# Sample attention of a hybrid layer: keys transposed in 32x32 blocks on VectorE, scores by sixteen 32x32 TensorE tiles

## The chip, the cores and the metric

The kernel runs on one core of a Trainium2 chip. The metric is the time of one launch in microseconds on the device. The engines are named as in the profile: PE is TensorE, PEld its weight loads, DVE is VectorE, ACT is ScalarE, POOL is GpSimd, SP is SyncE.

## What is computed

One layer of a hybrid decoder: 1024 prompt tokens and 8 sample sequences of 8 new tokens each. Half of the mixing width is gated linear attention (GLA), half is multi-head latent attention (MLA) with 4 heads, 256 latent channels and 64 rotary ones; then an output projection and a gated convolutional FFN. The change lies in one part, the attention of the sample tokens over a paged cache of 8192 rows per sequence:

```python
s = einsum('bthl,bsl->bhts', ql, kv) + einsum('bthr,bsr->bhts', qr, kr)
p = softmax(s * scale)
o_lat = einsum('bhts,bsl->bthl', p, kv)
# b 8 sequences, t 8 tokens, h 4 heads, s 8192 keys, l 256, r 64, all float32
```

## The kernel before

The program has four stretches: norms and input projection (to about 318 us of the trace), a mixed stretch, then output projection and FFN (from about 966 us). In the mixed stretch two generators are run side by side: `mla_sample` (lines 1143 to 1235) and `main`, which does the prompt's queries, then GLA, then the prompt's attention. Each yields a number that stands for its share of the work, and whoever is behind goes next. A scheduler of the framework then fixes the order of the instructions of every engine when the program is built; each engine runs its own queue in that order and waits on semaphores.

`mla_sample` runs over 8 sequences and 4 steps each, 32 steps in all, of 2048 keys in two halves. Per half, POOL issues two gathers: L, 128 partitions by 8 keys by 256 latent channels (line 1166, five buffers), and R, the 64 rotary channels of the same keys (line 1167, three buffers). PE transposes L and R in 20 blocks of 128x128 (line 1176) into the PSUM tile kps (two buffers), four blocks to a bank, and ACT copies each bank to KT or KR (line 1178). The scores S fill one bank: the 32 queries (4 heads by 8 tokens) times 512 keys for each quarter of the keys' partitions, four quarters on the 128 partitions, by four column tiles of 128x32 (lines 1186 and 1188). DVE takes the maximum of each partition (rm, line 1191), brings the four quarters together (mg, lines 1194 and 1198) and writes one negated maximum per query back to all quarters (nm, line 1201). ACT takes the exponential p (line 1204) and the factor al for the old sums (line 1207). DVE transposes p in 32x32 blocks (pt, line 1215), PE multiplies by L in 16 products of 128x32 (O, line 1220), and DVE adds to the running sum (on, lines 1223 and 1225). A sequence ends with two small products that add the quarters (fps and lps). float32 products of TensorE appear in the trace as two records each, transposes as one.

KT, KR and S have one buffer each, but O has a bank of its own, so the keys of a step are transposed while the step before still is at its exponentials and O.

Of the kernel before, what the change touches and what calls it, by code (L numbers as in the profile page):

```python
# [10 lines left out]
F32 = mybir.dt.float32  # L11
# [3 lines left out]
AF = mybir.ActivationFunctionType  # L15
# [24 lines left out]
def _consts():  # L40
# [24 lines left out]
    # the rows of a modulation: four parts of nine in steps of 32, then the bias  # L65
# [28 lines left out]
class Rows:  # L94
    """the transposes of all tokens' rows, in two parts each, by groups of tokens"""
# [10 lines left out]
class Kernel:  # L106
# [128 lines left out]
    def ada_section(self, sec, wp, pp, bufs, evac, rp=None):  # L235
# [9 lines left out]
                # four products side by side  # L245
# [60 lines left out]
    def gate(self, k, gvec, gp, name, gb):  # L306
        """gate rows times the norm's gain, for prompt and sample tokens: [128, 2, 1024]"""
# [18 lines left out]
    def to_T(self, xp, pp, xn, h, i, slot, nraw=3, eng=None, both=None):  # L326
        """xn: the normalized rows of tile i; their transposes, modulated, into h"""
# [24 lines left out]
    def phase1(self):  # L352
# [3 lines left out]
        with ExitStack() as es:  # L356
# [37 lines left out]
            # the sample tokens' two parts side by side  # L394
# [22 lines left out]
            def gates():  # L417
                """the forget gates"""
# [18 lines left out]
            def ada():  # L437
                """the other parts of the modulation, a little after each of the products"""
# [19 lines left out]
            # low-rank gate input and query latent  # L458
# [20 lines left out]
            # latents and rotary keys  # L479
# [24 lines left out]
            # GLA queries and keys, transposed  # L504
# [19 lines left out]
            # indices of the sixteenths of pages, by partition  # L524
# [8 lines left out]
            # values and output gates  # L533
# [18 lines left out]
    def rope(self, xp, out, x, tab, h):  # L552
        """out, x: [n, h, 64]; tab [n, 2, 64]"""
# [42 lines left out]
    def gla_group(self, G, cp, bp, pm, g):  # L596
# [16 lines left out]
        # the forget gates' running sums within blocks  # L613
# [11 lines left out]
        # intra-block scores, by levels  # L625
        # odd blocks of 64 on the upper partitions, where their values are
# [54 lines left out]
        # decayed queries and keys  # L681
# [60 lines left out]
        # output norm and gate  # L742
# [7 lines left out]
    def head_norm(self, bp, o, m, nh, gg=None):  # L750
        """o [m, x, y] in place: rows of 128 normalized, times gg [128, 128] if given"""
# [11 lines left out]
    def gla_sample(self, cp, pm, qe, ke, dec, v, at2, o_sb):  # L763
# [9 lines left out]
        # the sums of even and odd sequences side by side  # L773
# [29 lines left out]
    def outer(self, out, k, v):  # L803
        """the heads' sums of keys times values, two heads side by side"""
# [15 lines left out]
    def mla_weights(self, mp, pp):  # L820
# [5 lines left out]
        # the first head's first  # L826
# [77 lines left out]
    def sample_queries(self, zs, xs, ds, es2):  # L904
        """the sample tokens' queries, and the prompt's last ones"""
# [819 lines left out]
```

## Time and profile before

| what | value |
|---|---|
| median of 3 runs | 1889.26 us (1887.93 to 1892.58) |
| the profiled execution, its own time as the trace gives it, first to last instruction (span) | 1894.2 us |
| PE busy | 1815.7 us, 96% |
| DVE, ACT, POOL busy | 939.5, 709.2, 527.4 us |
| mean granted clock of TensorE | 0.984 |

The time of an engine is the sum of what it was busy with, not of what it held up; the views by window, by line and by time tell these apart. PE rows and PEld rows overlap. PE's busy time counts a matmul from its start to its end, and pipelined matmuls overlap, so the time that a group of products takes is best read from the timeline, where a run of them stands as one row.

### The profile page before, as it was taken

Reading aid. Unit: us, or ns where it says so; the run is one execution under the profiler, and the core shown is the slowest. Engines: PE = TensorE matmul, PEld = TensorE weight load, DVE = VectorE, ACT = ScalarE, POOL = GpSimd, SP = SyncE. Lnnn points to the kernel's source line nnn. Section 1 sums busy time; section 2 is a strip of 40 time slices with the busy share of each in tenths; the row PEclk is TensorE's granted clock in tenths of the full one; section 3 lists DMA queues with packets and bytes.
Section 4 is the critical chain, followed back from the end, with each engine's and each line's share of the span. In section 5 each row is a group of like instructions: output and inputs, shape, how many; then the busy total and the mean of one; then the engine's idle time right before and its main releaser. Section 6 shows DMA issues by size and latency. Waiting matters only on the chain.

```text
span 1894.2 us, 30775 instructions
## 1 busy us (share of the span) xinstructions
PE 1815.7 (96%) x12403; PEld 1502.5 (79%) x12403; DVE 939.5 (50%) x1680; ACT 709.2 (37%) x1398; POOL 527.4 (28%) x567
## 2 busy tenths in 40 slices
PE   6999999998998899999999999999999999999998
PEld 3888767764555567776679999999999999888787
DVE  4740334355676445554557755555555554623433
ACT  3451112464456556756633422222222222323322
POOL 2640101243334323232102123333333332202221
PEclk8999999999989999999999999999999999999999
DMA  8155553565454744545445331111121212744563
GB/s 312 68 171 180 187 160 111 192 206 180 169 183 159 250 160 150 188 138 180 159 145 176 101 98 68 61 64 63 68 70 69 70 62 70 246 115 114 155 188 94
DMA packets 170617, 265.26 MB, mean 140 GB/s; under 512 B 18277, under 2 KB 118693, under 8 KB 162282
## 3 DMA queue, kind: packets, MB, share of 16 engines
q1 hardware_dynamic: 156138, 179.39, 29.6%
q0 software_dynamic: 14336, 83.89, 12.7%
q8 instruction: 98, 1.61, 0.3%
q14 instruction: 45, 0.37, 0.1%
HBM read 221.49 MB, written 41.75 MB: 139 GB/s over the span
## 4 chain that ended last, share of the span: by engine, by line
PE 83%; DVE 6%; DMA 5%; ACT 3%; issue 2%; POOL 1%; SPq 1%; DVEq 0%; POOLq 0%; ACTq 0%
PE ups L140 9%; PE ups L142 9%; PE ups L141 9%; PE kps L1176 6%; PE yps L142 4%; PE yps L140 4%; PE yps L141 4%; PE zps L140 3%; PE O L1220 3%; PE zps L142 3%; PE zps L141 3%; PE S L1186 3%; PE y L142 2%; PE y L140 2%; PE y L141 2%
## 5 line engine op out<-in xcount | busy, mean ns | idle before, releaser
L140 PE MATMUL ups<-gh,uhi 128*128 128x384 f32 (+1 forms) x1056 | 347.2, 329 | 0.3 <-DVE hraw L343 0.3
L141 PE MATMUL ups<-gl,uhi 128*128 128x384 f32 (+1 forms) x1056 | 346.7, 328 | 0.0
L142 PE MATMUL ups<-gh,ulo 128*128 128x384 f32 (+1 forms) x1056 | 346.5, 328 | 0.0
L1514 DVE TENSOR_SCALAR cv<-u,vt 128x1024 f32<-128x1024 f32 (+1 forms) x88 | 133.2, 1534 | 216.3 <-ACT u L1504 179.4
L140 PEld LDWEIGHTS ups<-gh,uhi 128*128 128x128 f32 x1056 | 198.3, 188 | 0.7 <-DVE hraw L343 0.6
L142 PEld LDWEIGHTS ups<-gh,ulo 128*128 128x128 f32 x1056 | 198.3, 188 | 0.1
L141 PEld LDWEIGHTS ups<-gl,uhi 128*128 128x128 f32 x1056 | 198.3, 188 | 0.0
L1176 PE MATMUL kps<-ident,L 128*128 128x128 f32 x1024 | 159.9, 286 | 22.4 <-ACT KT L1178 16.2
L1178 ACT COPY KT<-kps 128x512 f32<-128x512 f32 x256 | 145.8, 590 | 82.8 <-PE kps L1176 77.5
L1176 PEld LDWEIGHTS kps<-ident,L 128*128 128x128 f32 x1024 | 113.8, 143 | 78.8 <-issue 42.5
L121 POOL TENSOR_TENSOR ulo<-uraw,uhi 128x2048 fp32r<-128x2048 f32 x24 | 111.4, 4642 | 207.5 <-ACT uhi L1342 204.6
L1504 ACT COPY u<-ups 128x384 f32<-128x384 f32 (+1 forms) x130 | 57.6, 444 | 279.2 <-PE ups L142 279.2
L142 PE MATMUL yps<-uhi,gl 128*128 128x512 f32 x341 | 133.3, 392 | 5.0 <-DVE gl L121 5.0
L140 PE MATMUL yps<-uhi,gh 128*128 128x512 f32 x341 | 133.1, 391 | 0.0
L141 PE MATMUL yps<-ulo,gh 128*128 128x512 f32 x341 | 133.0, 390 | 0.0
L121 DVE TENSOR_TENSOR gl<-graw,gh 128x1408 fp32r<-128x1408 f32 x31 | 59.1, 1908 | 129.3 <-ACT gh L1561 129.3
L1167 POOL DMA_INDIRECT R<-cache_krope,idx x64 | 66.1, 1033 | 181.6 <-PE kps L1176 148.5
L1342 ACT CAST uhi<-uraw 128x2048 fp32r<-128x2048 f32 (+1 forms) x38 | 70.8, 1865 | 94.4 <-PE ups L141 66.9
L1561 ACT CAST gh<-graw 128x1408 fp32r<-128x1408 f32 (+1 forms) x35 | 45.8, 1310 | 158.1 <-PE yps L141 128.6
L1166 POOL DMA_INDIRECT L<-cache_latent,idx x64 | 61.5, 961 | 138.9 <-PE O L1220 68.4
L140 PE MATMUL zps<-whi,hh 128*128 128x512 f32 (+2 forms) x256 | 96.1, 375 | 0.0
L142 PE MATMUL zps<-whi,hl 128*128 128x512 f32 (+2 forms) x256 | 94.2, 368 | 0.8 <-DVE hl L121 0.8
(443 smaller groups left out, 3799.1 us busy)
## 6 DMA issues: line engine op xcount, KB each, us to landing
wraw<-w_ada SPq DMA_DIRECT2D x48, 512.0 KB
uraw<-w_ffn_up SPq DMA_DIRECT2D x22, 1024.0 KB
graw<-s_g SPq DMA_DIRECT2D x32, 704.0 KB
s_g<-gl SPq DMA_DIRECT2D x22, 544.0 KB
uraw<-w_ffn_down SPq DMA_DIRECT2D x10, 1024.0 KB
xt<-x_prompt SPq DMA_DIRECT2D x16, 512.0 KB
wraw<-w_in SPq DMA_DIRECT2D x12, 512.0 KB
uraw<-w_o SPq DMA_DIRECT2D x4, 1024.0 KB
```

Source lines behind the costliest of these rows:

```text
L121: eng.tensor_tensor(out, x, hi.bitcast(F32), ALU.subtract)
L140: mm(out, wh, xh, start=start, stop=False)
L141: mm(out, wh, xl, start=False, stop=False)
L142: mm(out, wl, xh, start=False, stop=stop)
L1166: nc.gpsimd.indirect_dma_start(L.rearrange("p j l -> p (j l)"), None, cl, io)
L1167: nc.gpsimd.indirect_dma_start(R.rearrange("p j l -> p (j l)"), None, ck, io)
L1176: nc.tensor.transpose(ps[:, k], x, self.ident)
L1178: nc.scalar.copy(KT[:, q // 2, j0:j0 + 4] if q < 4 else KR[:, 4 * half:4 * half + 4], ps)
L1186: nc.tensor.matmul(S[r], Q[:, c], KT[:, c, :, r], start=(c == 0), stop=False)
L1342: self.nc.scalar.copy(hi, raw)
L1504: copy(u[:, 2 + c0:2 + c0 + m], ps[:, 0:m])
L1514: nc.vector.tensor_scalar(yv[z], sh(2)[z], self.cw2[:, ch:ch + 1], self.cb[:, ch:ch + 1], ALU.mult, ALU.add)
```

## The change

The keys are no longer transposed on PE. DVE transposes L and R where they lie, in blocks of 32x32, by three instructions per half (lines 1177 and 1179 of the changed file): 128x1024 elements twice, 128x512 once. After this, partition 32x+i holds channel 32c+i of the keys that lay on partitions 32x to 32x+31, for ten chunks c of 32 channels. The queries are laid out to match: Qd holds, for each of the ten chunks, the same 32 rows on all four partition groups; it is made once, by twelve products with a replicating matrix `rep` and twelve copies. The scores are then sixteen tiles of 32x32 for each chunk (x the row group and the PSUM bank, g the column group), 160 products of 128 columns per step, into four banks.

The maximum is kept for each of the 128 partitions by itself: a reduction with negation (line 1192) and, from a sequence's second step, a minimum with the old one (line 1194); mg and its copies leave the step. p is transposed on PE by four 128x128 transposes (line 1210) with one ACT copy (line 1212). O is as before, with another order of the products. At the end of each sequence the four quarters' maxima are brought together, and their factor f scales the selecting matrix (lines 1228 to 1246).

The pools: S now is a tile of four banks with one buffer, and the transposed p, O and the end of the sequence are tiles of the same tag, so they use the same four banks one after the other. kps and its two banks are gone. L has six buffers instead of five, R two instead of three, and KT three (of a half each) instead of one.

```diff
+            rep = dq.tile([P, 4, 4, 32], F32, name="rep")
+            nc.vector.tensor_copy(rep, self.ident.rearrange("p (x o a) -> p x o a", x=4, o=1).broadcast_to([P, 4, 4, 32]))
...
+            for c in range(8):
+                ps = pq.tile([P, 4, 8, 8], F32, name="qps", tag="Q")
+                nc.tensor.matmul(ps.rearrange("p h b t -> p (h b t)"), rep[:, c % 4], qs[:, c // 4].rearrange("p h n -> p (h n)"), start=True, stop=True)
+                (nc.vector.tensor_copy if c % 2 else nc.scalar.copy)(Qd[:, c].rearrange("p b h t -> p h b t"), ps)
...
-                    for q in range(5):
-                        ps = psK.tile([P, 4, P], F32, name="kps", tag="K")
-                        for k in range(4):
-                            x = L[:, 4 * (q % 2) + k, q // 2 * P:q // 2 * P + P] if q < 4 else R[:, 2 * k:2 * k + 2].rearrange("p j r -> p (j r)")
-                            nc.tensor.transpose(ps[:, k], x, self.ident)
-                        j0 = 8 * half + q % 2 * 4
-                        nc.scalar.copy(KT[:, q // 2, j0:j0 + 4] if q < 4 else KR[:, 4 * half:4 * half + 4], ps)
-                        yield 0.5
+                    K = bp.tile([P, 10, 8, 32], F32, name="KT", tag="KT", bufs=3)
+                    for h in range(2):
+                        j = slice(4 * h, 4 * h + 4)
+                        nc.vector.transpose(K[:, 0:8, j].rearrange("p c j k -> p j c k"), L[:, j].rearrange("p j (c k) -> p j c k", k=32))
+                        yield 1.0
+                    nc.vector.transpose(K[:, 8:10].rearrange("p c j k -> p j c k"), R.rearrange("p j (c k) -> p j c k", k=32))
+                    yield 0.5
...
+                S = psS.tile([P, 4, 512], F32, name="S", tag="S")[:, :, 0:P]
+                for c in range(10):
                     for g in range(4):
-                        r = slice(32 * g, 32 * g + 32)
-                        if c < 2:
-                            nc.tensor.matmul(S[r], Q[:, c], KT[:, c, :, r], start=(c == 0), stop=False)
-                        else:
-                            nc.tensor.matmul(S2[r, c - 2], Q[:, c], KR[:, :, r], start=False, stop=(c == 3))
+                        for x in range(4):
+                            r = slice(32 * x, 32 * x + 32)
+                            nc.tensor.matmul(S[32 * g:32 * g + 32, x], Q[r, c], Ks[g // 2][r, c, 4 * (g % 2):4 * (g % 2) + 4].rearrange("p j k -> p (j k)"),
+                                             start=(c == 0), stop=(c == 9))
...
+                nc.vector.tensor_reduce(nm, S, AX.XY, ALU.max, negate=True)
+                if nmo is not None:
+                    nc.vector.tensor_tensor(nm, nm, nmo, ALU.min)
...
-                nc.vector.transpose(pt, p)
+                SO = psS.tile([P, 4, 512], F32, name="S", tag="S")
+                pps = SO[:, 0].rearrange("p (j q) -> p j q", j=4)
+                for j in range(4):
+                    nc.tensor.transpose(pps[:, j], p[:, j], self.ident)
+                nc.scalar.copy(pt, pps)
+                O = SO[:, 1, 0:LAT]
```

How the queues stand, in the stretch beside the prompt's attention. PE's queue of the kernel before, around the scores of one step (kps, S and O belong to the sample attention; sps, pt and olps are the prompt's scores, its transposed weights and its products with the latents):

```order
L1176 MATMUL kps<-ident,R 128x128 x4
L1186 MATMUL S<-KT,Qd 32x512 x4
L1176 MATMUL kps<-ident,L 128x128 x4
L1122 MATMUL pt<-ident,ol 128x128 x2
L1188 MATMUL S<-KR,Qd 32x8x32 x8
L1176 MATMUL kps<-ident,L 128x128 x8
L1107 MATMUL pt<-ident,p 128x128 x3
L1176 MATMUL kps<-ident,L 128x128 x4
L1176 MATMUL kps<-ident,R 128x128 x4
```

The scores of a step stand there in pieces, with transposes of the next keys and work of the prompt between them. PE's queue of the changed kernel at such a place, with all 160 products of a step in a row:

```order
L1086 MATMUL sps<-causal,identr 128x128
L140 MATMUL olps<-pth,vh 128x256
L1187 MATMUL S<-KT,Qd 32x128 x160
L141 MATMUL olps<-ptl,vh 128x256
L142 MATMUL olps<-pth,vl 128x256
L140 MATMUL olps<-pth,vh 128x256
L141 MATMUL olps<-ptl,vh 128x256
L142 MATMUL olps<-pth,vl 128x256
L1114 MATMUL pt<-ident,p 128x128 x3
```

Further on in the same step come the four transposes of p and then O, with the prompt's products between them:

```order
L140 MATMUL olps<-pth,vh 128x256
L1210 MATMUL S<-ident,p 128x128 x4
L141 MATMUL olps<-ptl,vh 128x256
L142 MATMUL olps<-pth,vl 128x256
L140 MATMUL olps<-pth,vh 128x128
L141 MATMUL olps<-ptl,vh 128x128
L142 MATMUL olps<-pth,vl 128x128
L1218 MATMUL S<-L,pt 32x256 x16
```

What moved: the keys' transposes are gone from between the prompt's products, the scores stand in one block, and the prompt's products that follow a block wait behind it. The number of products in a row differs from step to step; in the steps beside GLA the block is also cut in places. GLA's last work stands in the twelfth step of the changed order, and the last two steps have next to no work of `main` beside them.

DVE's queue of the kernel before, over one step:

```order
L1191 TENSOR_REDUCE rm<-S 128x1
L1194 COPY mg<-rm 32x1 x4
L1198 TENSOR_REDUCE mg<-mg 32x1
L1201 TENSOR_SCALAR nm<-mg 32x1 x4
L1091 SCALAR_TENSOR_TENSOR ls<-ls,al,l_8149 128x1
L121 TENSOR_TENSOR ptl<-pt,pth 128x384
L1081 TENSOR_REDUCE nm<-sps 128x1
L1215 STREAM_TRANSPOSE pt<-p 128x512
L1081 TENSOR_REDUCE nm<-sps 128x1
L1209 SCALAR_TENSOR_TENSOR ln<-ln,al,rs 128x1
```

DVE's queue of the changed kernel from the first half's transposes of a step to the sum ln:

```order
L1177 STREAM_TRANSPOSE KT<-L 128x4x8x32 x2
L1179 STREAM_TRANSPOSE KT<-R 128x8x2x32
L1192 TENSOR_REDUCE nm<-S 128x1
L1177 STREAM_TRANSPOSE KT<-L 128x4x8x32 x2
L1179 STREAM_TRANSPOSE KT<-R 128x8x2x32
L1132 TENSOR_TENSOR ob<-pt,ri 128x256
L1194 TENSOR_TENSOR nm<-nm 128x1
L121 TENSOR_TENSOR Kl<-sps,Kh 128x512 x2
L757 TENSOR_REDUCE hms<-hsq 128x2
L1202 SCALAR_TENSOR_TENSOR ln<-ln,al,rs 128x1
```

What moved: the six transposes of the keys stand three before the reduction over S and three behind it, ahead of the minimum that ACT's exponential waits for; the copies of the maxima and the transpose of p are gone.

## Rows read from the trace of the kernel before

**Rows 1.** The page: engines' busy time over the span; then the view of cores.

```profile
PE 1815.7 (96%) x12403; PEld 1502.5 (79%) x12403; DVE 939.5 (50%) x1680; ACT 709.2 (37%) x1398; POOL 527.4 (28%) x567
...
core 0: 1894.2 us, clock 0.984
```

**Rows 2.** Windows: start:end, length, busy us (instructions) of each engine, clock, DMA share, GB/s.

```profile
318.00:405.00 87.00, 81.05 (x681) 62.91 (x679) 35.26 (x111) 41.72 (x92) 28.94 (x28) 0.98 0.59 199
405.00:630.00 225.00, 201.15 (x2085) 125.98 (x2088) 142.03 (x361) 127.22 (x274) 87.60 (x97) 0.95 0.53 179
630.00:966.00 336.00, 320.30 (x2756) 223.26 (x2744) 172.10 (x492) 201.08 (x484) 86.81 (x112) 0.99 0.51 173
```

**Rows 3.** Lines, 318 to 966 us, old transposes, their copies, scores: count, busy us, mean ns, idle.

```profile
L1176 PE MATMUL kps<-ident,L 128*128 128x128 f32 x1024 | 159.9, 286 | 22.4 <-ACT KT L1178 16.2 <-ACT KR L1178 2.6 <-issue 1.7
L1176 PE MATMUL kps<-ident,R 128*128 128x128 f32 x256 | 42.2, 289 | 1.1 <-ACT KT L1178 0.9
L1178 ACT COPY KT<-kps 128x512 f32<-128x512 f32 x256 | 145.8, 590 | 82.8 <-PE kps L1176 77.5 <-PE O L1220 2.0 <-issue 0.9
L1178 ACT COPY KR<-kps 128x512 f32<-128x512 f32 x64 | 37.7, 588 | 26.3 <-PE kps L1176 26.2
L1186 PE MATMUL S<-KT,Qd 128*32 128x512 f32 x512 | 75.4, 611 | 0.6 <-ACT p L1204 0.6
L1188 PE MATMUL S<-KR,Qd 128*32 128x256 f32 x512 | 40.9, 385 | 0.0
```

**Rows 4.** Lines, same stretch: the maximum, the transposed weights, and O's matmuls and loads.

```profile
L1191 DVE TENSOR_REDUCE rm<-S 128x1 f32<-128x512 f32 x32 | 22.0, 686 | 22.2 <-PE S L1188 18.4 <-PE kps L1176 3.7
L1194 DVE COPY mg<-rm 32x1 f32<-32x1 f32 x128 | 18.1, 142 | 2.0
L1198 DVE TENSOR_REDUCE mg<-mg 32x1 f32<-32x5 f32 (+1 forms) x32 | 4.6, 144 | 0.9
L1201 DVE TENSOR_SCALAR nm<-mg 32x1 f32<-32x1 f32 x128 | 18.4, 144 | 2.2
L1215 DVE STREAM_TRANSPOSE pt<-p 128x512 f32<-128x512 f32 x32 | 22.7, 710 | 14.1 <-ACT p L1204 12.9 <-ACT KT L1178 0.8
L1220 PE MATMUL O<-L,pt 128*32 128x256 f32 x1024 | 68.8, 387 | 2.6 <-DVE pt L1215 1.6 <-issue 0.8
L1220 PEld LDWEIGHTS O<-L,pt 128*32 128x32 f32 x1024 | 31.3, 110 | 27.5 <-issue 5.9 <-DVE pt L1215 3.2 <-ACT KT L1178 0.4
```

**Rows 5.** Timeline, 784 to 798 us: start, duration, engine, operation [idle before].

```profile
784.64 0.71 ACT L1204 ACTIVATE p<-S,nm 128x512 f32<-128x512 f32 x1
785.47 0.71 DVE L1215 STREAM_TRANSPOSE pt<-p 128x512 f32<-128x512 f32 x1
787.10 1.93 PE L1220 MATMUL O<-L,pt 128*32 128x256 f32 x32
788.97 1.09 PE L1176 MATMUL kps<-ident,L 128*128 128x128 f32 x8
789.16 0.48 DVE L1225 SCALAR_TENSOR_TENSOR on<-on,al,O 128x256 f32<-128x256 f32 x1 [1.29 <-PE O L1220]
790.73 0.66 PE L1176 MATMUL kps<-ident,L 128*128 128x128 f32 x4 [0.45 <-issue]
793.04 1.07 PE L1186 MATMUL S<-KT,Qd 128*32 128x512 f32 x8
797.35 1.07 PE L1188 MATMUL S<-KR,Qd 128*32 128x256 f32 x16
```

**Rows 6.** Timeline of PE at 477 us: 64x64 tiles on two row groups and two column groups.

```profile
477.01 1.09 PE L716 MATMUL ops<-v,att 64*64 64x128 f32 x16
```

**Rows 7.** The instructions of two lines on DVE that take 1024 columns: min/median/max ns.

```profile
L323 DVE TENSOR_SCALAR rt<-xt,rstd x9: 739/747/754, 997.0 to 1094.7; 128x1024 f32<-128x1024 f32 x8, 64x1024 f32<-64x1024 f32 x1
...
L1428 DVE TENSOR_TENSOR xt<-rt,xt x9: 1208/1218/1226, 993.3 to 1089.3; 128x1024 f32<-128x1024 f32 x8, 64x1024 f32<-64x1024 f32 x1
```

**Rows 8.** Windows: the stretch with the lowest clock among these stages.

```profile
440.00:560.00 120.00, 104.10 (x1118) 67.31 (x1114) 81.81 (x195) 60.77 (x126) 43.79 (x47) 0.90 0.50 173
```

More of the change, by code (lines that the diff above doesn't have):

```diff
@@ L1181, in mla_sample @@
-                S2 = S.rearrange("p (j two k) -> p two j k", two=2, k=32)
-                for c in range(4):
-                    for g in range(4):
-                        r = slice(32 * g, 32 * g + 32)
-                        if c < 2:
-                            nc.tensor.matmul(S[r], Q[:, c], KT[:, c, :, r], start=(c == 0), stop=False)
-                        else:
-                            nc.tensor.matmul(S2[r, c - 2], Q[:, c], KR[:, :, r], start=False, stop=(c == 3))
-                yield 4.4
@@ L1190, in mla_sample @@
-                rm = bp.tile([P, 1], F32, name="rm", tag="rm")
-                nc.vector.tensor_reduce(rm, S, AX.X, ALU.max)
-                mg = mnext or bp.tile([32, 5], F32, name="mg", tag="mg", bufs=3)
-                for g in range(4):
-                    nc.vector.tensor_copy(mg[:, g:g + 1], rm[32 * g:32 * g + 32])
-                first = pc == 0
-                mnext = bp.tile([32, 5], F32, name="mg", tag="mg", bufs=3)
-                mnew = mnext[:, 4:5]
-                nc.vector.tensor_reduce(mnew, mg[:, 0:4 if first else 5], AX.X, ALU.max)
+                    K = bp.tile([P, 10, 8, 32], F32, name="KT", tag="KT", bufs=3)
@@ L1206, in mla_sample @@
+                if nmo is not None:
                     al = bp.tile([P, 1], F32, name="al", tag="al")
@@ L1212, in mla_sample @@
                     lrun = rs
[L1213 to L1220 removed]
+                nmo = nm
+                SO = psS.tile([P, 4, 512], F32, name="S", tag="S")
+                pps = SO[:, 0].rearrange("p (j q) -> p j q", j=4)
+                for j in range(4):
+                    nc.tensor.transpose(pps[:, j], p[:, j], self.ident)
+                pt = bp.tile([P, 4, P], F32, name="pt", tag="pt")
+                nc.scalar.copy(pt, pps)
+                O = SO[:, 1, 0:LAT]
+                for j in range(4):
+                    for g in range(4):
+                        r = slice(32 * g, 32 * g + 32)
+                        nc.tensor.matmul(O[r], pt[:, j, r], Ls[g // 2][:, 4 * (g % 2) + j], start=(j == 0), stop=(j == 3))
                 on = bp.tile([P, LAT], F32, name="on", tag="on")
@@ L1227, in mla_sample @@
                 yield 4.0
-            fps = psV.tile([P, 2, 32], F32, name="fps", tag="O")
+            mg = bp.tile([32, 5], F32, name="mg", tag="mg")
+            for g in range(4):
+                nc.scalar.copy(mg[:, g:g + 1], nmo[32 * g:32 * g + 32])
+            nc.vector.tensor_reduce(mg[:, 4:5], mg[:, 0:4], AX.X, ALU.min)
+            nM = bp.tile([P, 1], F32, name="nM", tag="nM")
+            for g in range(4):
+                nc.scalar.copy(nM[32 * g:32 * g + 32], mg[:, 4:5])
+            f = bp.tile([P, 1], F32, name="f", tag="f")
+            nc.scalar.activation(f, nmo, AF.Exp, scale=-1.0, bias=nM)
+            sel = bp.tile([P, 32], F32, name="sel", tag="sel")
+            nc.vector.tensor_scalar(sel, self.small[:, SELG], f, None, ALU.mult)
+            fin = psS.tile([P, 4, 512], F32, name="S", tag="S")
+            fps = fin[:, 0, 0:64].rearrange("p (a q) -> p a q", a=2)
             for a in range(2):
-                nc.tensor.matmul(fps[:, a], oacc[:, a * P:(a + 1) * P], self.small[:, SELG], start=True, stop=True)
+                nc.tensor.matmul(fps[:, a], oacc[:, a * P:(a + 1) * P], sel, start=(a == 0), stop=(a == 1))
             nc.scalar.copy(od[:, :, :, b], fps.rearrange("p a (h t) -> p a h t", t=8))
-            lps = psV.tile([32, 1], F32, name="lps", tag="O")
-            nc.tensor.matmul(lps, self.small[:, SELG], lrun, start=True, stop=True)
+            lps = fin[0:32, 1, 0:1]
+            nc.tensor.matmul(lps, sel, lrun, start=True, stop=True)
             nc.scalar.copy(ML[:, 1, b:b + 1], lps)
-            nc.scalar.copy(ML[:, 0, b:b + 1], mrun)
+            nc.scalar.mul(ML[:, 0, b:b + 1], mg[:, 4:5], -1.0)
     def mla_merge(self, psV):
```

42 lines of the change are left out of this document (14 added, 28 removed).

## The prediction

> **What bounds the kernel now.** I read the page first, then the cores, then windows by stretch, then lines and the timeline inside the one stretch that the change touches. PE is busy 1815.7 us of the span of 1894.2 us, at a mean granted clock of 0.984 [rows 1], so in most places PE's queue sets the time. The change touches 318 to 966 us, and there three stages follow one another: the prompt's queries (87 us), GLA (225 us) and the prompt's attention (336 us), 648 us together. PE is busy 81.05, 201.15 and 320.30 us in them, DVE only 35.26, 142.03 and 172.10 us [rows 2]. The reader is to see that PE is nearly full in the last stage, that GLA has 24 us of gaps, and that DVE has room in all three, least in GLA (63%). By the starts of the 32 transposes of p [rows 4], 3, 11 and 18 of the steps fall into the three stages. Everything behind 966 us is untouched and keeps its time, so the forecast is the sum of the three stages against 648 us.
>
> **What PE loses and gains.** Transposes of the keys: a row of four lasts 0.66 us, one of eight 1.09 us [rows 5], so one more transpose costs (1.09 - 0.66)/4 = 0.108 us; 40 a step are 4.3 us, 138 us in 32 steps. (The mean of 286 ns in [rows 3] counts overlapped matmuls whole and would say three times as much.) The old scores: two rows of eight at 1.07 us and one of sixteen at 1.07 us [rows 5], 3.2 us. The new scores are 160 products, 320 records of 128 columns. If sixteen tiles run side by side these are 20 waves, and one pass of 128 columns costs about what a transpose does, 0.108 us: 2.2 us, and with 0.3 us for filling and draining 2.5 us. That is the value I take. It is unmeasured here: the nearest rows are four column tiles (O: 32 records of 256 columns in 1.93 us, 60 ns each [rows 5]) and two row groups on two column groups (sixteen records of 128 columns in 1.09 us, about 0.2 us more than 8 x 0.108 [rows 6], so the two do run at once). Below, the bound is 20 x 0.108 = 2.2 us; above, at O's rate with half the columns, 320 x 27 ns = 8.6 us, as if row groups that share a column group took turns. I stay near the lower end because rows 6 show row groups side by side, though on different columns.
>
> Added on PE: four transposes of p, 0.6 us a step (the row of four, pipelined into its neighbours), and once some 4.5 us for Qd (24 records of 256 or 128 columns, 0.1 to 0.2 us each). PE's net is -4.3 - 0.7 + 0.6 = -4.4 us a step.
>
> The weights of these tiles are loaded 32x32 at a time. In O, 32 loads of 110 ns [rows 4] fit into 1.93 us together with 32 products [rows 5], which is no more than 8 waves of 0.24 us, so loads lie behind running products there. The Trainium skill, "TensorE: Matmul & The Clock Gate", section "Part 3: Packing small matmuls — row/col tiling", says that a weight load overlaps running matmuls only where its row group differs. By that rule the loads of O, which use the same rows as the products before, would have to wait, and the trace shows that they do not. What it would make of the time stands below as a rival. The same section gives 10.6 times for sixteen tiles; as an estimate from that figure, 320 x 0.108/10.6 = 3.3 us, and the total would be some 20 us above mine; no run here shows it.
>
> **What ACT loses and gains.** Ten copies of 0.59 us a step go, 183.5 us in all [rows 3]; one of the same size comes (p transposed, 0.59 us). ACT was not the bound, but kps waited for it: PE's 22.4 us idle before transposes, mostly for KT's copies [rows 3], go with them.
>
> **What DVE gains.** A transpose of 128x512 takes 710 ns [rows 4]. For 128x1024 the rows of that size are 747 ns and 1218 ns [rows 7]; twice the smaller transpose is 1.42 us. A transpose at the first row's rate would take half of 0.71 us at 512 columns, which it does not, so I take 1.24 us, beside the second row; the bounds are 0.75 and 1.42. A step has 4 x 1.24 + 2 x 0.71 = 6.4 us of them and a minimum of one column (0.15, like the small operations of [rows 4]); the copies, the small reduction, nm and the transpose of p go: 0.57 + 0.14 + 0.57 + 0.71 = 2.0 us. Net +4.6 us a step, +146 us, and DVE's 349 us in these stages become 496 us.
>
> **Where it lies.** Before, the next step's keys were transposed while a step was at p and O, since O had its own bank. Now S, p's transpose and O share one buffer of four banks, so a step's scores start only when on of the step before is done, and in DVE's queue three transposes stand between the reduction and the minimum (the order excerpts of the change). A step becomes one chain: scores 2.5, reduction 0.69, three transposes 3.2, minimum 0.15, p 0.71, its transpose 0.63, copy 0.59, O 1.93, on 0.48: 10.9 us. For hops: before, p to the end of on took 789.64 - 784.64 = 5.0 us, of which 3.83 us was work [rows 5], so 0.39 us for each of three hops; eight hops are 3.1 us. A sequence's end (a small chain of maxima, f and two products, some 1.5 us) is 0.4 us a step, and 0.9 us stand for products of the prompt queued ahead of O and of S. The chain is 15.3 us.
>
> What fills it: PE has 2.5 + 0.6 + 1.9 = 5 us of sample work a step and the prompt's work in between. In the order of the change GLA ends in the twelfth step, so about 20 steps lie beside the prompt's attention, 10 beside GLA, the rest before. The gathers stay hidden: POOL is busy 26 to 39% [rows 2], but R, with two buffers, now waits for DVE's transposes and L for O six buffers back.
>
> **The sum.** Queries: 87 - 3 x 4.4 + 4.5 = 78, taken as 79. GLA: PE would need about 160 us, but DVE gets 142 + 10 x 4.6 = 188 us minus 4 for the step that moves into the next stage; with DVE at 93% of it, a share that I choose as near full, about 198 us. Prompt's attention: PE's 320 us lose 18 x 4.4 = 79, so the chain decides, 20 x 15.3 = 306 us. Together 583 instead of 648: -65 us. On the profiled execution that is 1894.2 - 65 = 1829 us; the median of the runs is 1889.26 us, 5 us lower, and I put the forecast at **1826 us** (own range 1790 to 1875: S from 2.2 to 4 us, the lower third of its bounds, hops from 0.2 to 0.6 us). The clock is a smaller unknown: it was lowest, 0.90, where PE was busy only 104 of 120 us [rows 8], so a PE with gaps can lose some of its gain.
>
> **Rivals.**
> - *PE alone bounds, the waits are covered.* With hops of 0.15 us and no queueing the chain is 10.9 + 1.2 + 0.4 = 12.5 us, the last stage is PE's or the chain's, about 250 to 260 us, GLA 193: 532, -116, about **1775 us**. For it: the old stage kept PE at 95% despite its chain [rows 2]. Against: one S buffer forbids two steps at once. Chance 0.14.
> - *Sixteen tiles do not run at once.* Tiles that share a column group take turns, the scores cost 8.6 us: the chain 21.4 us, 20 x 21.4 = 428, GLA 240, queries 97: 765, **about 2005 us**. For it: no row here shows two row groups on one column group. Against: rows 6. Chance 0.09.
> - *A tile's next weights wait for its running product.* A wave is then 0.108 + 0.110 us [rows 4], the scores 4.4 us, 1.9 us more a step; 20 steps beside the prompt's attention and part of the others give some 48 us: **about 1875 us**. Against: O's loads, above. Chance 0.04. This is the rule of the page named above, from "TensorE: Matmul & The Clock Gate" of the Trainium skill.
> - *The single buffer's chain is the bound, slower.* Nothing is wrong with a price, but each hop waits longer: PE and DVE run their queues in order, a chain instruction stands behind the prompt's work, and the prompt's work behind a chain instruction that waits. It decides from 648/32 = 20.2 us a step on. With 1.0 us a hop instead of 0.39, and 2.5 us instead of 1.3 for the ends and the queue, it is 10.9 + 8.0 + 2.5 = 21.4 us: 32 x 21.4 = 685, +37, **about 1928 us**. For it: GLA's own chain already leaves gaps of 24 us. Against: the measured 0.39. Chance 0.13.
> - *DVE transposes from strided tiles at half the rate.* The keys' transposes write runs of 32 elements, the old one wrote a flat tile. Then DVE gets 6.4 us more a step, 496 + 205 = 701 us of 648, and the stretch follows it: **about 1955 us**. Against: both move the same 32x32 blocks. Chance 0.05.
> - *It comes out even*, the chain eating exactly what PE gives: 0.07.
>
> **How the numbers follow.** The forecast has 0.48. A measurement here can tell about 0.3% (6 us) from no change. Faster by more: 0.48 + 0.04 + 0.14 = 0.66; within: 0.07; slower: 0.13 + 0.09 + 0.05 = 0.27. The range 1765 to 1945 holds the forecast, the waiting weights, the even case, the long chain and most of the first rival; the tiles in turns and the slow transposes lie outside, with some of the first, about 0.18.
>
> **What would show it.** In the profile after: L1177 128 times at about 1.24 us, L1179 64 times at 0.71; a row of 320 records of L1187 of about 2.5 us; DVE near 496 us and PE near 465 us between 318 us and the end of the sample attention, which should come near 900 us; waits of PE for on (L1223) and of ACT's p for the minimum (L1194). It is wrong if scores last over 5 us, if steps beside the prompt's attention are more than 18.6 us apart ((648 - 79 - 198)/20, from where nothing is gained), or if they are 12 us apart with PE full.

## The result, and the profile after

The changed kernel takes 2187.43 us (median of 4 runs, 2185.05 to 2196.6) where the kernel before takes 1888.99 us: a ratio of 1.1585, with a 95% interval of 1.1567 to 1.1603. It is 298 us slower; 1826 us were forecast.

The page's first part of the changed kernel, its instruction queue in part 3, and the view of cores, beside [rows 1]:

```profile
span 2194.8 us, 46593 instructions
PE 1896.0 (86%) x20491; PEld 1575.1 (72%) x20491; DVE 1061.2 (48%) x1592; ACT 579.4 (26%) x1188; POOL 529.2 (24%) x567
...
q8 instruction: 160, 2.62, 0.5%
...
core 0: 2194.8 us, clock 0.888
```

The same lines of the kernel before say 30775 instructions and, for that queue:

```profile
q8 instruction: 98, 1.61, 0.3%
```

PE is no longer full, and its mean granted clock has fallen from 0.984 to 0.888. The kernel has 15818 more instructions, and queue q8 moved 62 more packets, 1.01 MB: by division 64 bytes an instruction and 16 KB, or 256 instructions, a packet. By windows, for the queries, GLA and the prompt's attention, beside [rows 2]:

```profile
318.00:405.00 87.00, 67.69 (x970) 54.49 (x969) 43.68 (x90) 23.42 (x56) 24.44 (x23) 0.90 0.49 176
405.00:650.00 245.00, 167.17 (x3734) 114.90 (x3737) 154.20 (x283) 67.76 (x165) 75.53 (x83) 0.72 0.41 136
650.00:1266.00 616.00, 446.96 (x8895) 313.82 (x8887) 280.74 (x508) 154.55 (x420) 105.62 (x132) 0.74 0.35 116
```

The three stages take 948 us instead of 648, the whole loss; 79, 198 and 306 us were forecast, 87, 245 and 616 came. So nearly all of the miss lies beside the prompt's attention, where 22 steps start 28.3 us apart. There PE is busy for 73% of the time, at a granted clock of 0.74. The stretch behind 1266 us takes 929 us, as before.

The lines, beside [rows 3] and [rows 4]:

```profile
L1187 PE MATMUL S<-KT,Qd 32*32 32x128 f32 x10240 | 226.9, 317 | 116.3 <-issue 111.6 <-DVE on L1223 2.8 <-DVE on L1221 1.1
L1177 DVE STREAM_TRANSPOSE KT<-L 128x1024 f32<-128x1024 f32 x128 | 151.1, 1218 | 116.7 <-PE S L1187 115.9 <-issue 0.6
L1179 DVE STREAM_TRANSPOSE KT<-R 128x512 f32<-128x512 f32 x64 | 42.9, 670 | 0.0
L1218 PE MATMUL S<-L,pt 128*32 128x256 f32 x1024 | 79.5, 463 | 9.4 <-ACT pt L1212 9.4
```

The transposes cost what was forecast (1.22 and 0.67 us). Three things were not forecast. Inside the scores PE is idle for 111.6 us with "issue" as the reason: it waits for nothing that the profile shows. DVE's first transposes of a step wait 115.9 us for the scores. And the 32 blocks of scores stand in 138 pieces: 18 are whole, and 85 of the 106 cuts lie beside the prompt's attention and 9 beside GLA, where alone the text on the change had them. The timeline of PE (start, duration, [idle before]) has both ways in which the scores go wrong, in cut blocks and in whole ones:

```profile
902.96 0.63 PE L1187 MATMUL S<-KT,Qd 32*32 32x128 f32 x2
904.04 0.63 PE L1187 MATMUL S<-KT,Qd 32*32 32x128 f32 x2
905.11 0.63 PE L1187 MATMUL S<-KT,Qd 32*32 32x128 f32 x2
...
911.66 0.42 PE L141 MATMUL olps<-ptl,vh 128*128 128x256 f32 x1
911.87 0.41 PE L142 MATMUL olps<-pth,vl 128*128 128x256 f32 x1
...
930.32 3.44 PE L1187 MATMUL S<-KT,Qd 32*32 32x128 f32 x240
936.26 1.89 PE L1187 MATMUL S<-KT,Qd 32*32 32x128 f32 x80 [2.50 <-issue]
```

Between the rows at 902.96 and 904.04 stands one product of the prompt: 1.07 us for both, where such a product takes 0.21 us in a row of its kind (911.66 to 911.87); the granted clock is 0.50 at both places. At 930.32, 240 of 320 records start 13.3 ns apart, then PE stands for 2.5 us. No packet of q8 moves from 930.5 to 934; one does between 934 and 935.1. The same holds all over: each of the 38 gaps of over 0.5 us inside the scores ends 2.2 to 3.1 us after a packet of q8 began.

The chain of waits, in order of time (start, duration, what), from the last score of a step:

```profile
1037.61 1.26 PE S L1187 x46
1038.89 2.37 DVE KT L1177 x2
1041.26 0.59 DVE KT L1179
1041.85 0.57 DVE nm L1192
1042.43 2.27 DVE KT L1177 x2
1044.70 0.59 DVE KT L1179
```

All six transposes of this step lie behind its scores, three ahead of the reduction and three ahead of the minimum. (A sequence's first step has no minimum.)

By the starts and ends of S, p, O and `on` in the trace, a step beside the prompt's attention is one chain, as forecast: the next scores start 1.7 us after `on` in the mean. The scores, from first to last, take 13.1 us of the 28.3, where the forecast had 2.5 of 15.3; from the last score to the exponential are 5.9 us. Of the 13 us that a step is longer than forecast, the scores, with what stands in their cuts, hold over 10.

### The profile page after: what moved, and what is told of

The parts are those of the page before. It is cut to its first block, busy times and chain, and to the rows that moved or that the text cites. A ratio compares the mean times of both kernels' runs of the same rounds, so it can differ in the third digit from the quotient of the medians.

```text
span 2194.8 us, 46593 instructions
## 1 busy us (share of the span) xinstructions
PE 1896.0 (86%) x20491; PEld 1575.1 (72%) x20491; DVE 1061.2 (48%) x1592; ACT 579.4 (26%) x1188; POOL 529.2 (24%) x567
## 4 chain that ended last, share of the span: by engine, by line
PE 55%; DVE 6%; issue 4%; ACT 1%; DMA 1%; SPq 0%; DVEq 0%; POOLq 0%; ACTq 0%; POOL 0%
PE ups L140 8%; PE ups L142 8%; PE ups L141 8%; PE S L1187 6%; PE yps L142 3%; PE yps L140 3%; PE yps L141 3%; DVE KT L1177 3%; PE S L1218 2%; PE y L140 1%; PE y L141 1%; PE y L142 1%; PE sps L140 1%; PE pt L1114 1%; DVE KT L1179 1%
## 5 line engine op out<-in xcount | busy, mean ns | idle before, releaser
L1187 PE MATMUL S<-KT,Qd 32*32 32x128 f32 x10240 | 226.9, 317 | 116.3 <-issue 111.6
L1187 PEld LDWEIGHTS S<-KT,Qd 32*32 32x32 f32 x10240 | 148.9, 112 | 167.1 <-issue 142.3
L1177 DVE STREAM_TRANSPOSE KT<-L 128x1024 f32<-128x1024 f32 x128 | 151.1, 1218 | 116.7 <-PE S L1187 115.9
L141 PE MATMUL zps<-wlo,hh 128*128 128x512 f32 (+2 forms) x256 | 93.2, 364 | 0.0
```

The costliest lines, as they stand in the source:

```text
L141: mm(out, wh, xl, start=False, stop=False)
L1177: nc.vector.transpose(K[:, 0:8, j].rearrange("p c j k -> p j c k"), L[:, j].rearrange("p j (c k) -> p j c k", k=32))
L1187: nc.tensor.matmul(S[32 * g:32 * g + 32, x], Q[r, c], Ks[g // 2][r, c, 4 * (g % 2):4 * (g % 2) + 4].rearrange("p j k -> p (j k)"), start=( ...
```

## The experiments

Times are medians; the kernel before, run beside each of them, took 1888 to 1894 us. Runs without an interval are single ones and are read for differences of tens of us only. Every edit also moves the order that the scheduler gives to the queues, and e10 shows below that such a shift alone can be worth 40 us.

**Whole blocks (e1).** The scores get a priority that keeps a step's 160 products together in PE's queue.

```diff
+                pri = self.tc.cur_priority
+                self.tc.cur_priority = pri - 3000
                 S = psS.tile([P, 4, 512], F32, name="S", tag="S")[:, :, 0:P]
...
+                self.tc.cur_priority = pri + 161
```

> All 160 products of every step stand in one row of PE's queue, nothing else changes. In the changed kernel 85 of the score runs beside the prompt's attention are single products between the prompt's own; one such change there and back takes 1.07 us where the prompt's product alone takes 0.22. Theory cuts: these changes of tile shape lie on PE's path: 85 x 0.85 = 72 us less, about 2115 us. Theory fetch (PE runs out of instructions inside a block of scores; 124 us of gaps in the profile): the gaps stay, and since the cut steps had given time to fetch, a part of the gain is lost: 2130 to 2170 us. Theory chain (the single buffer of four banks and the hops set the step): within 20 us of 2187.

2155.36 us, 32 less. The gaps inside the scores grew, from 111.6 to 128.8 us, as theory fetch has it, and took back part of what the cuts cost. (By the trace there are 85 cuts beside the prompt's attention, and 61 single products among the pieces.)

```profile
PE S L1189 <- issue: 128.8, 43, 5.1
```

**Half and twice the instructions (e2, e3).** As many columns in 80 products of 256 and in 320 of 64. With 256 columns the kernel leaves out half of the chunks of channels from the scores, here and in e6, e9 and e13.

```diff
-                for c in range(10):
+                for c in range(5):
...
-                            nc.tensor.matmul(S[32 * g:32 * g + 32, x], Q[r, c], Ks[g // 2][r, c, 4 * (g % 2):4 * (g % 2) + 4].rearrange("p j k -> p (j k)"),
+                            nc.tensor.matmul(S[32 * g:32 * g + 32, x, 0:2 * P], Q[r, c], Ks[g // 2][r, c].rearrange("p j k -> p (j k)"),
```

> Half the products, each with 256 columns instead of 128: as many columns, half the instructions. It leaves five of the ten chunks of channels out of the scores. Theory fetch: 320 instructions per step fit into what PE has at hand, the gaps of 2 to 6 us inside the scores go, a step's scores take about 2.5 us instead of 4.3 plus gaps: 32 x (1.8 + 3.9) = 180 us less, about 2005 us, and the granted clock rises. Theory tiles in turns (columns set the time, as if tiles of one column group waited for each other): scores as long as before, 2170 to 2190 us. Theory weights wait (a tile's next load waits for its product): 10 waves of 0.216 + 0.11 us = 3.3 us, 1 us less a step; with the gaps unchanged about 2150 us.

> Twice the products, each with 64 columns: as many columns, twice the instructions, the same result. Theory fetch: 1280 instructions a step, 640 records at 13.5 ns = 8.6 us and two or three more blocks of 16 KB to wait for at 2 to 4 us: 9 to 13 us more a step, 290 to 410 us more, 2480 to 2600 us. Theory tiles in turns: no change but for the loads, 2190 to 2260 us. Theory chain: the chain gets longer by what the scores get longer, as in fetch, so this run does not part those two.

2109.76 and 2422.05 us: 78 less and 235 more. Both go the way of theory fetch and by less than it said; in e2 17 of 32 blocks are still cut. "Tiles in turns" falls: with as many columns the time moves by over 300 us. The timeline of PE in e3 shows the supply at work:

```profile
845.10 1.95 PE L1189 MATMUL S<-KT,Qd 32*32 32x64 f32 x128 [4.14 <-issue]
849.94 1.95 PE L1189 MATMUL S<-KT,Qd 32*32 32x64 f32 x128 [2.89 <-issue]
853.68 1.95 PE L1189 MATMUL S<-KT,Qd 32*32 32x64 f32 x128 [1.79 <-issue]
```

128 records and their 128 loads are 256 instructions, one packet of 16 KB. PE runs through one in 1.95 us and stands for 1.8 to 4.1 us until it has the next. How long it stands goes with what else the DMA engines carry. Queues in the gaps ahead of 845.10 and 857.43:

```profile
q0 software_dynamic: 192, 1.42, 94.7%
...
q1 hardware_dynamic: 12, 0.01, 2.4%
```

Of the 122 gaps of over 0.5 us in e3, the 92 in which the DMA engines are under 20% busy have a mean of 1.8 us, the other 30, most of them under the gathers of q0, 3.5 us. This holds for a step's first gap (1.5 and 3.4 us) as for later ones (1.8 and 4.0). No run takes the gathers away, so that they delay the instructions is likely and not shown.

**Whole blocks with half the instructions (e6).** Both edits together.

> Uncut blocks and half the instructions with twice the columns (five of ten chunks of channels are left out of the scores). Of a step of 24.9 us with uncut blocks, 9.5 us were scores; here they took 3.0. Theory fetch and cuts (they account for what the forecast missed but for some 3 us a step): 24.9 - 6.5 = 18.4 us a step, 2155 - 32 x 6.5 = 1947 us, or less if the clock rises with it. Theory chain alone: the other waits take over, 21 us a step, 2050 us or more.

2029.39 us: 126 less than e1, between the two expectations. The gaps are gone, and a step's scores are one row of 3.4 us. That also answers "tiles in turns" directly: it has 8.6 us for these columns.

```profile
PE S L1189 <- issue: 1.7, 3, 0.8
...
953.26 3.39 PE L1189 MATMUL S<-KT,Qd 32*32 32x256 f32 x160
```

The time is 82 us above what the fetch theory gave for this run, so other waits do take over in part.

**The maximum alone (e4, e5, e10, e11, e16).** In the kernel before, the maximum per partition, p transposed on PE, and the merge at a sequence's end; keys and scores stay as they were.

```diff
-                rm = bp.tile([P, 1], F32, name="rm", tag="rm")
-                nc.vector.tensor_reduce(rm, S, AX.X, ALU.max)
...
+                nc.vector.tensor_reduce(nm, S, AX.X, ALU.max, negate=True)
+                if nmo is not None:
+                    nc.vector.tensor_tensor(nm, nm, nmo, ALU.min)
...
-                            nc.tensor.matmul(S[r], Q[:, c], KT[:, c, :, r], start=(c == 0), stop=False)
+                            nc.tensor.matmul(S[r], Q[:, c], KT[:, c, 4 * g:4 * g + 4].rearrange("p j k -> p (j k)"), start=(c == 0), stop=False)
```

> The kernel before with the other half of the change alone: keys and scores by 128x128 transposes and 128x32 tiles as before, a maximum per partition, p transposed on PE, merged at a sequence's end. If the maximum's part is harmless, as my sum has it (PE +0.6, DVE -2.6 us a step, a shorter chain, its own banks): 1870 to 1895 us. If the p transposes on PE and the merges cost on the path: up to 1920 us.

2044.79 us, and a bad test: each column tile now needs other copies of the keys, so the four tiles of a chunk stand apart in PE's queue. The scores' busy time shows that they run at once no longer, 178.3 us against 75.4 us in [rows 3]:

```profile
L1186 PE MATMUL S<-KT,Qd 128*32 128x512 f32 x512 | 178.3, 605 | 0.0
```

e5 groups them (tile g takes `KT[:, c, g::4]`):

> The kernel before with the change's maximum alone, as in the run of that name, but the four column tiles take key slots g, g+4, g+8, g+12, so that all four need the same copies and stand together in the queue; in the first such run the tiles stood one or two at a time between the prompt's products, and the scores' busy time went from 75 to 178 us. If that was the loss of 156 us: 1870 to 1905 us. If the maximum itself (p transposed on PE and copied by ACT ahead of O) was: again about 2045 us.

1945.09 us. The scores are back at 71.1 us, and PE now waits 24.3 us for p and 7.5 us for its copy:

```profile
PE kps L1207 <- ACT p L1195: 24.3, 18, 3.3
```

e10 adds to e5 the change's arrangement, scores, p's transpose and O in one tile with one buffer, as the cost to be added (the fence is against e5). e11 gives e5's transpose of p back to DVE; the weights then meet the keys in another order, so it computes something else:

```diff
-                pps = psK.tile([P, 4, P], F32, name="kps", tag="K")
+                SO = psS.tile([P, 2, 512], F32, name="S", tag="S")
+                pps = SO[:, 0].rearrange("p (j q) -> p j q", j=4)
...
-                O = psV.tile([P, LAT], F32, name="O", tag="O")
+                O = SO[:, 1, 0:LAT]
```

> The kernel with the maximum's part alone and grouped tiles (1945 us), and now scores, transposed p, O and the sequence's end share one PSUM tile with one buffer, as in the change; keys, scores and everything else stay. Theory shared buffer: the next step's scores can't start before on of this one; PE's queue stands behind them, some 2 to 4 us a step, 2010 to 2070 us. If PE has enough other work ahead of the scores (the key transposes stand there, unlike in the change): within 15 us of 1945.

> The kernel with the maximum's part alone and grouped tiles (1945 us), but p is transposed in 32x32 blocks by DVE as before the change, with no transpose on PE and no copy by ACT; the weights then meet keys in another order, which part of the computation it changes. Theory (the 56 us over the kernel before are PE's four transposes a step, 0.6 us, and PE's wait for p and for ACT's copy, 36 and 12 us of loads' idle time in its profile): back to 1880 to 1900 us. If the loss is elsewhere (the merges at the sequences' ends, the other order of O): 1920 to 1945 us.

1904.22 and 1904.27 us. The suspected cost is a gain of 41 us: with the shared buffer the order of PE's queue comes out other, and its wait for p falls from 24.3 to 5.3 us. e10 has all of e5's parts, so e5's 56 us are no fixed price of them; that the order made them is read from the waits. e10 again, four times:

> e10 again with rounds, to tell whether the maximum's part with the shared buffer is slower than the kernel before at all (1904 in one look, beside 1894 of the kernel before in the same call). Theory harmless: ratio 1.000 to 1.006. Theory that the single buffer costs: 1.01 or more.

1902.35 us, a ratio of 1.0069 (1.0046 to 1.0093). The maximum's part with its shared buffer costs some 13 us (14 by the medians), a little more than "harmless" allowed.

**Key buffers (e7, e9).** Four half-step buffers of keys instead of three, and for the room five of L instead of six.

```diff
-                    K = bp.tile([P, 10, 8, 32], F32, name="KT", tag="KT", bufs=3)
+                    K = bp.tile([P, 10, 8, 32], F32, name="KT", tag="KT", bufs=4)
```

> Uncut blocks, four half-step buffers of transposed keys instead of three (five of L instead of six for the room). DVE's queue then has four of the six transposes ahead of the step's reduction, and only one of R between reduction and minimum. Theory chain: the 2.4 us of two transposes leave each step's chain, 25 to 32 steps: 60 to 75 us less than 2155, about 2085 us. If the chain is not what bounds (PE's gaps for instructions are): within 20 us of 2155.

2096.47 us, 59 less than e1, as theory chain has it; from a step's last score to its exponential the mean is 4.8 us, in e1 6.2. But the room taken from L shows too: DVE now waits for gathers, 89.9 us.

```profile
DVE KT L1177 <- DMA L<-cache_latent,idx: 89.9, 29, 8.9
```

> Uncut blocks, half the instructions with twice the columns (five of ten chunks of channels left out of the scores) and four key buffers, all at once. If the three effects are separate and add up: 2187 - 32 (uncut) - 126 (instructions, 2155 to 2029) - 59 (key buffers, 2155 to 2096) = 1970 us. If they cover each other (DVE's transposes hide behind the gaps, or the reverse), 2000 to 2030 us. Below 1889 us would say that the small tiles' instructions and DVE's place in the queue are the whole loss; what stays above it belongs to the maximum's part (p through PE and ACT), the shared buffer and the clock.

2080.11 us, 51 more than e6 and a miss of every expectation. Here DVE waits 97.5 us for gathers of L, in e6 2.6. So the lost buffer of L may cost more than the fourth key buffer gives; this run does not part them.

**A block-diagonal layout (e8).** Keys by DVE, queries on the diagonal of a 128x128 tile, 20 products a step; two buffers for S and for O, and the maximum of the kernel before.

```diff
+                    for c in range(10):
+                        nc.tensor.matmul(S[:, 256 * half:256 * half + 256], Q[:, c].rearrange("p x q -> p (x q)"), K[:, c].rearrange("p j k -> p (j k)"),
+                                         start=(half == 0 and c == 0), stop=(half == 1 and c == 9))
```

> The keys by DVE as in the change, but the queries laid out block-diagonal in a 128x128 tile: one product per chunk and half, K = 128 rows, 128 columns, 256 moving: 20 products (40 records) a step instead of 160 (320), no small tiles, no change of tile shape; S is one bank, two buffers, O has its own, and maximum, p and O are those of the kernel before. PE: 40 x 0.108 = 4.3 us instead of 4.3 + 3.2 of before, -3.2 us a step; DVE: +6.4 us a step, 349 + 205 = 554 of 648 us. Theory (the small tiles' instructions, their cuts and the single buffer caused the loss, not the transposes on DVE): 1830 to 1900 us. If DVE's transposes alone lengthen the path: 1950 us or more.

2020.33 us, 1.0692 (1.0668 to 1.0715), in the range given for DVE's transposes alone lengthening the path. But the expectation priced a record of 256 columns like one of 128, and the trace has twice that:

```profile
800.94 4.48 PE L1186 MATMUL S<-KT,QB 128*128 128x256 f32 x20
```

At this rate 40 records are 9 us, more than the 7.5 us of transposes and scores that they replace. So this run does not single out DVE; it says that a loss of 131 us stays without any small tile.

**Reduction and minimum first (e12, e13).** On top of whole blocks (e1), a one-column copy from the running maximum into a key buffer orders DVE's queue.

```diff
+                    if len(nms) >= 2 - half:
+                        nc.vector.tensor_copy(K[:, 0, 0, 0:1], nms[half - 2])
```

> Uncut blocks as in e1 (2155 us), and the transposes that refill a key buffer get a one-column copy from the running maximum ahead of them, so that DVE does the reduction and the minimum of a step first and the transposes behind them; two more copies of 0.14 us a step. Theory chain (DVE's six transposes lie between scores and exponential): 6.1 us a step leave the chain, less where GLA's own chain decides: 20 to 30 steps, 120 to 180 us less, 1975 to 2035 us. Theory PE's supply of instructions alone: within 20 us of 2155.

> The same with half the instructions and twice the columns (five of ten chunks of channels left out of the scores), beside e6 (2029 us). If chain and instructions add up: 2029 - 120 to 180 = 1850 to 1910 us, the kernel before or better. If the granted clock (0.81 in e6's stages) holds it: 1920 to 1980 us.

2100.48 us (55 less than e1) and 1972.53 us (57 less than e6). With e1 and e6 this is a square of four single runs: the order is worth 55 and 57 us, halving the instructions 126 and 128, whatever the other is. Both effects are clear of the noise, and they add up. The order's worth is less than half of what was expected, and e13 ends in the range that its expectation gave to the clock; no run tests that. In both runs a transpose of R, and in most steps one of L too, still stand ahead of the reduction. From the last score to the exponential the mean falls from 6.2 (e1) to 3.1 us (e12), while DVE's wait for the scores stays, 182.9 and 179.1 us: the edit takes transposes out of the chain, not this wait.

**Two blocks (e14).** e12 with the scores of a step in two parts of 80 and other products between. In the trace 13 of 32 steps still have them in one row.

```diff
+                    if c == 5:
+                        self.tc.cur_priority = pri + 81
+                        yield 2.2
+                        pri = self.tc.cur_priority
+                        self.tc.cur_priority = pri - 450
```

> e12 with each step's 160 products in two blocks of 80, in 21 of 32 steps with the prompt's or GLA's products between them, in the others together or cut. Theory supply: 320 instructions in a row leave no gap (e6 had 6 us of them in all), other work runs while the next are fetched: the 4.3 us of gaps go in 15 to 20 steps, 60 to 90 us less than e12, less what the further changes of tile shape cost (0.85 us each, some 40 more). If the gaps are not a matter of supply: as e12 or slower.

2062.99 us, 37 less than e12. The gaps inside the scores fall from 120.6 to 82.1 us, as if the next instructions arrived during the other products; cutting into two gains, where the change's cutting into small pieces lost.

**DVE's load alone (e15).** The kernel before with the six transposes of a step added, their results unused.

```diff
+                    K = bp.tile([P, 10, 8, 32], F32, name="KD", tag="KD", bufs=2)
+                    for h in range(2):
+                        j = slice(4 * h, 4 * h + 4)
+                        nc.vector.transpose(K[:, 0:8, j].rearrange("p c j k -> p j c k"), L[:, j].rearrange("p j (c k) -> p j c k", k=32))
+                    nc.vector.transpose(K[:, 8:10].rearrange("p c j k -> p j c k"), R.rearrange("p j (c k) -> p j c k", k=32))
```

> The kernel before, unchanged in all its work, with the change's six DVE transposes per step added (their results are not used): 205 us more on DVE and nothing else. My sum put DVE's load on no path beside the prompt's attention by itself. If DVE's load is harmless where nobody waits for it: within 20 us of 1889. If small instructions of the softmax chains of GLA, prompt and samples queue behind transposes of 1.2 us: 30 to 90 us more, 1920 to 1980, which would be the part of the 84 us that e13 still lies above the kernel before.

1957.81 us, 69 more. DVE is far from full (267 of 380 us beside the prompt's attention), but every chain of this stretch passes through its queue. PE waits in a dozen places a little longer; these two are among the longest:

```profile
PE lps L669 <- DVE Bb L662: 17.0, 8, 5.2
...
PE olps L141 <- DVE ptl L121: 8.4, 11, 2.5
```

Before, they were 8.4 and 1.4 us. The test is not pure: PE's queue has another order than before, and DVE stands 32.7 us at the added transposes until a gather has landed, with everything behind it. So the 69 us are load, order and this wait together. No version here beats the kernel before.

## Why the prediction was wrong

The mechanism was right in that beside the prompt's attention the chain of one step decides. Its terms were wrong, the scores' above all: 306 us were forecast for that stage, 20 steps of 15.3, and 616 came. Both of the prediction's own signs of being wrong came true, scores of over 5 us and steps more than 18.6 us apart.

Measured one by one: halving the instructions of the scores gives back 126 to 128 us, DVE's load costs 69, the place of the transposes in DVE's queue 55 to 57, cut blocks 32, the maximum with the shared buffer 13. That these sum up to 295 to 299 us, and the loss is 298, proves nothing: half of the instructions is not all of them, the load was measured on the kernel before and in another order, and the work that PE lost is not in the sum.

- **The step that failed first is the price of the scores**, 2.5 us a step as 20 waves of 0.108 us. The 18 whole blocks take 5.9 to 11.9 us by the starts of their first and last records, 9.5 in the mean. It has two parts. A pair of load and product takes 13.3 ns (the row of 240 at 930.32, by starts), which is 4.3 us for 320; the forecast had little more than half of that. And 640 instructions come in a burst that outruns their supply, 4.2 us of gaps in the mean of the whole blocks. The prediction counted columns, not instructions; no row of the kernel before has so many in so short a time, and the mean lies above even its upper bound of 8.6 us. That instructions are the cause, and not columns, is shown by e1 against e6 and by e3.
- **The rival of the waiting weights had the pair's price**, at a chance of 0.04. It gives 0.218 us for a wave of sixteen, 13.6 ns a pair, and for 256 columns (0.216 + 0.11)/16 = 20.4 ns; by the starts of the records the rows have 13.3 and 18.9 ns (e6, 953.26). For 64 columns it gives 10 ns and e3's row has 12.9, so something else sets the pace there. The rival follows the rule of "TensorE: Matmul & The Clock Gate" of the Trainium skill, "Part 3: Packing small matmuls — row/col tiling", that a load overlaps running products only where the row group differs. Taken as the rival took it, for a tile's own product alone, the small tiles come near it at two of three widths, while O's tiles before did not agree with it [rows 4, 5]. Why the two kinds differ stays open.
- **DVE's prices were right**, and its place on the path was in part wrong. The chain had three transposes between scores and minimum, as if the three ahead of the reduction had been done during the scores. They need a key buffer that only the step's last score frees: 115.9 us of DVE's waits. Most steps have six in the chain, 6.1 us instead of 3.2. In e12 and e13, where only some of them leave it, this gives 55 to 57 us.
- **DVE's load got no term** beside the prompt's attention. e15 has 69 us for it in a kernel where nobody waits for these transposes, with a changed order of the queues in it.
- **The cuts** were read in the order, as a thing of the steps beside GLA, and left out of the sum. The trace has 85 beside the prompt's attention. A single product costs some 0.85 us of PE at the lower clock, and e1 gains 32 us in all after what the supply takes back.
- **The clock** was called a smaller unknown. In two stages it was 0.72 and 0.74. The O of a step, 1.93 us in [rows 5], takes twice that in such places:

```profile
382.05 3.64 PE L1218 MATMUL S<-L,pt 128*32 128x256 f32 x32 [0.67 <-ACT pt L1212]
...
382.00:386.00 4.00, 3.95 (x35) 1.76 (x35) 0.71 (x3) 0.00 (x1) 0.98 (x2) 0.50 0.38 121
```

  Granted is 0.50 there, so of the two levels it is 1.2 instead of 2.4 GHz, here behind 3.09 us in which PE waited for p. No run holds the clock fixed, so its share is inside the parts above and is not told apart.
- **The rival of the long chain** said that the single buffer's chain would bound the step, with every price right and longer hops. The chain does bound it, but a price was wrong. e10 and e16 put the buffer with the maximum at 13 us where PE is full (e10: busy 324.57 of 336 us beside the prompt's attention). In the change PE is not full, and each step's scores start close behind `on` of the step before, so there the same buffer may cost more; no run gives these scores a second one. **The rival of tiles in turns** had the time nearest to the measured one, about 2005 us, for a reason that e2, e3 and e6 refute.

One slip is beside the point: 5 us off 1829 are 1824, not 1826.

What stays open: which of load, order and clock hold the 84 us that e13 lies above the kernel before, and what a second set of banks for the scores would give.

## What to carry to other kernels

Price small tiles by the instruction as well as by the column: here a pair cost 13 ns with 64 columns as with 128. Whole blocks of 320 pairs all ran into the supply, after 122 to 261 pairs, and of e6's 31 whole blocks of 160 pairs two did. An engine with room to spare is not free: before giving it long instructions, look for the short ones of other chains that stand in the same queue, and for the buffer that each long one waits for. And when a part is tested alone, look at the order of the queues first: e4 and e5 lost 156 and 56 us, where the same parts in another order, with the shared buffer, cost 13 (e16).

## What was not expected of the hardware

By the counts above PE's instructions arrive in packets of 16 KB, 256 of 64 bytes; in e3 PE ran exactly 128 pairs, 1.95 us, and stood mostly for 1.5 to 2.1 us, at most 5.6, over and over. The gaps carry no name but "issue" in the profile, and were 111.6 us in the change, 268.6 us with twice the instructions (e3) and 1.7 us with half in whole blocks (e6). They were twice as long where the DMA engines had other transfers. A single 32x32 product between two 128x128 products costs 1.07 us there and back with the large product, against 0.21 us for the large product alone, both at a granted clock of 0.50; at 1139.59 us of the same trace, at 1.00, it costs 0.64 us.
